# One step of a hybrid decoder on one core: other blocks for three pieces of MLP side work, other results with stored low parts, weights and cache in DRAM in the order of their loads

## The chip, the core and the metric

The kernel runs on one core of one Trainium2 chip. The metric is the device time of one launch in microseconds (us). Names of engines as in the profile: PE is TensorE, which multiplies matrices; PEld is its weight load; DVE is VectorE; ACT is ScalarE; POOL is GpSimd; SP only issues transfers. Each engine works through its own queue in program order, and so do the DMA queues that SP, ACT and POOL issue to. "Granted clock" is the share of full speed at which PE was allowed to run.

## What is computed

A layer of a decoder on 576 rows (512 of a prompt and 8 x 8 sampled ones) of 2048 features, in float32. Cut to what matters:

```python
q, k, v, logf, u = mixer_inputs(x, g_mix, w_in, b_f)       # rms_norm(x) @ w_in, split
attn = attention of the prompt, or over 2048 cached positions for the sampled rows
x = x + concat([rms_norm(attn), conv_heads(u)]) @ w_out
hid = square(relu(rms_norm(x, g_mlp) @ w_up))              # 2048 -> 8192
x = x + hid @ w_down                                       # 8192 -> 2048
gate = sigmoid(rms_norm(x, g_ple) @ w_ple_gate)
x = x + (pe @ w_ple) * gate
y = rms_norm(x, g_final)
```

The cache is paged: `page_table` says which physical page holds which positions.

## The kernel before

**Precision.** Every float32 operand is split into a high part (ACT, `split_hi`, L152) and a low part, the rest (DVE, `split_lo`, L155). A product is three matmuls: high x high, high x low, low x high.

**Two phases.** `phase1` does the input projection, both attentions, the convolution and, through `outproj`, the output projection. `WStream` brings its weights in loads of [128, 4, 128] (256 KB). The cache comes in pages, one load of 256 KB each for K and V (L833). `phase2` is the MLP and the gate, and the change lies there for the most part. Its weights come through `QStream`: loads of two quads (512 KB) or one into `w2r` by SP's queue, three ahead, with four buffers; then sums for DVE (L1832 to L1834), the high part `w2h` on ACT and the low part `w2l` on DVE, three buffers each. `prep(t + 2)` issues these for the block two ahead.

**Blocks and segments.** The MLP's pass is a list of blocks t, written out in program order. A block takes one quad of weights (256 x 256) against one slot: an operand of 256 features in high and low parts (`xs`). Up (g = 1) and down (g = 2) use a scheme with 7 products instead of 8 for 2 x 2 tiles (`PRODS`), so a block is 21 matmuls (L1607 to L1609) into 7 PSUM banks of 8. A segment is a run of blocks with one result:
- up: 32 results p of 8 blocks each, t = 0 to 255;
- down: 8 results p, 32 operands k, in segments of a few operands (`DOWN_FIRST`, `DOWN_PART`); the first are (2, 0), (2, 1) and (2, 2) with 3 blocks each from t = 256, 259 and 262, then (2, 3) with 4 from 265. t = 256 to 511;
- gate: first (3, 0) with both halves of the rows, 8 blocks of 24 matmuls, t = 512 to 519; then (4, 1) to (4, 7) and (5, 1) to (5, 7), one half each, 12 matmuls a block.

**A segment's end.** `combine_head` takes the first products out of PSUM (ACT L1725, DVE L1726 and L1727, ACT L1728) and `combine_tail` the others, at the next segment's first block (L1738 to L1741). The next segment's second product needs the bank that L1725 frees, its third that of L1726. A segment of the gate ends with `plain_end` (L1685), which needs the norm's row `rb`.

**Side work.** What follows a result (`fin_up`, `fin_down`, `fin_gate`) and the splitting of the next slots (`build` in `mk`) are generators in the queues of `Beside`. After each block `run` takes steps from queue 0 and then queue 1 as long as a credit lasts; the credit grows by the block's time and falls by the estimated DVE time of what is issued. A step that yields -n lets n blocks pass before the next. `flush` forces a generator to its end. `hook(t, fn)` runs `fn` right after block t's matmuls are issued and ahead of that block's `run`. A slot's `work` that has not run when its block comes is flushed ahead of the block's `prep`. Queue 2 holds only the last up result's `fin_up`; `nudge` takes one step of it per block in segments of down with p = 1 and 2, from block 259 on, ahead of the bank copies of a segment's last block.

**`fin_up`**: scale by the norm (L1380), Relu and Square (ACT L1383, L1384), the sums T (DVE L1693 to L1696), stores by POOL to `down_in` (L1320 to L1322). For the results in `down_lo` also `low_rows`: the low parts are made (`lr`) and stored to `dl`.

**Ready operands.** The first four operands of down are loaded with both parts: `down_in` into the high half, `down_lo` into the low half (L1507, L1508), 1 MB each. What is left is the high split on ACT alone (two activations). `DOWN_K` sets which up results these are; `build` waits `min(now - firstuse + 4, -1)`, and a hook three blocks ahead of the first use flushes what is left (L1541).

**The final norm** of the MLP's output: `squares` adds up `acc2`; `row_rsqrt` then sums over partitions on PE (L182), takes the reciprocal root in a chain of small DVE instructions (L184 to L188), and spreads it by PE (L192, 512 and then 64 columns) and ACT copies (L193) into `rb2`. It is a generator that yields ahead of each of the two spreads. `fin_down(7)` puts it into queue 1 as `norm`, and the end of block 519 flushes it.

Of the kernel before, what the change touches and what calls it, by code (L numbers as in the profile page):

```python
# [21 lines left out]
KT = 16  # L22
# [10 lines left out]
READY = 4  # L33
DOWN_K = (*range(8, 8 + READY), *range(8), *range(8 + READY, 32))
FIRST_LOADS = 2, 4, 5, 6, 3
# [110 lines left out]
class Kern:  # L146
# [71 lines left out]
    def build(self):  # L218
        tc, nc, a = self.tc, self.nc, self.a
        with ExitStack() as top:  # L220
# [8 lines left out]
            self.down_in = [dram.tile([128, 7, HR], F32, name=f"di{j}") for j in range(32)]  # L229
            self.down_lo = {j: dram.tile([128, 7, HR], F32R, name=f"dl{j}") for j in DOWN_K[:READY]}  # L230
            cst = top.enter_context(tc.tile_pool(name="cst", bufs=1))
# [17 lines left out]
    def phase1(self):  # L249
# [20 lines left out]

        wt = lambda t: [a["w_main"][t][:, j:j + 4, :] for j in range(0, KT, 4)]
        order = [("q", 4), ("q", 5), ("q", 6), ("q", 7), ("k", 0), ("v", 0), ("k", 1), ("v", 1)]
# [7 lines left out]
        for t in range(KT):  # L280
            srcs += [a["w_out"][t][:, j:j + 4, :] for j in range(0, KT, 4)]
        self.ws = WStream(nc, w1, srcs)
# [538 lines left out]
    def kv_load(self, i, m):  # L821

        nc, a = self.nc, self.a
        while len(self.kv[i]) < min(m, 128):
            n = len(self.kv[i])
            G, c, w, j = n // 32, n // 8 % 4, n // 2 % 4, n % 2
            p = n % self.KVN[i] >= self.KVA
            t = self.kvp[p].tile([128, 2, 4, 128], F32, name="kv"[i], tag="kv"[i] * 2, bufs=self.KVN[i] - self.KVA if p else self.KVA)
            for x in range(2):
                b, pg = (w, 2 * j + x) if i == 0 else (2 * j + x, w)  # L830
                e = (G % 2 * 4 + b) * NPG + c * 4 + pg
                r = nc.sync.value_load(self.pti[0:1, e:e + 1])
                nc.sync.dma_start(t[:, x].rearrange("p h c -> p (h c)"),  # L833
                                  a["cache_kv"][bass.ds(r, 1), G // 2, :, 512 * i:512 * i + 512].rearrange("o p c -> p (o c)"))
            self.kv[i].append(t)
# [417 lines left out]
    def plan(self):  # L1253
# [12 lines left out]
        for g, p, k0, k1 in segs:  # L1266
            parts = [(k, min(2, k1 - k)) for k in range(k0, k1, 2)]
            if (g, p) == (1, 0):
                parts = [(0, 2), (2, 2), (7, 1), (4, 2), (6, 1)]
            for k, m in parts:  # L1270
                loads.append((wsrc[g][p][:, k:k + m], m, g >= 3))
            self.orders.append([k + i for k, m in parts for i in range(m)])
# [93 lines left out]
    def phase2(self):  # L1366
# [12 lines left out]
        def fin_up(p, c, r, final):  # L1379
            V(c, c, rbb, ALU.mult)  # L1380
            yield EL(2 * NR)
            yield -1
            nc.scalar.activation(c, c, AF.Relu)  # L1383
            nc.scalar.activation(c, c, AF.Square)  # L1384
            yield -1
            c, T = yield from self.operands(c, None)
            self.stored(c, T, self.down_in[p])
            if p in self.down_lo:
                yield from self.low_rows(c, T, self.down_lo[p])

        def fin_down(p, c, r, final):

            if not final:
                nc.gpsimd.dma_start(self.x1[p], c, accum_op=ALU.add)
                yield 0
                return
            V(c, c, r, ALU.add)
            yield EL(2 * NR)
            nc.gpsimd.dma_start(self.x2[p], c)
            yield -1  # L1400
            yield from self.squares(p, c)
            if p == 7:
                self.last_norm = bg.add(1, self.norm(self.P_))

# [86 lines left out]
        def mk(g, j, t=None, queue=nc.gpsimd):  # L1491
# [48 lines left out]
            if ready or late:  # L1540
                hook(firstuse[2, j] - 3, lambda: bg.flush(h.work))  # L1541

# [13 lines left out]
        for n in range(RING, len(seq)):  # L1556
            g, j = seq[n]
            at = max(at, lastuse[(2, 32 - RING + (2 * j + 1) // 3) if g == 3 else seq[n - RING]])
            if g == 3:
                at = max(at, segend[lastseg[g - 1, j]] + 1)  # L1560
            hook(at, lambda g=g, j=j: mk(g, j))
        places = {j: self.xslot() for j in range(2, 7)}
        self.last = self.xslot()
# [12 lines left out]
        for t, (si, k) in enumerate(quadlist):  # L1576
# [49 lines left out]
            if i == n - 1:  # L1626
                if g > 1:
                    bg.flush_all(0)
                if slow:
                    r = pre[g](p, lastseg[g, p] == si)  # L1630
                if (g, p) == (3, 0):
                    bg.flush(self.last_norm)
                if recent[0]:
# [245 lines left out]


def feat(v):

# [3 lines left out]
def layout(inp):  # L1886
# [8 lines left out]
    d["p"] = C(p.T.reshape(2, 128, 576).transpose(1, 0, 2))  # L1895
    d["w_main"] = C(wm.reshape(16, 128, 40, 128).transpose(2, 1, 0, 3))
    d["w_f"] = C(w[:, 3072:3080].reshape(16, 128, 8).transpose(1, 0, 2))
    wo = g["w_out"][0].reshape(8, 2, 128, 16, 128)[list(OUT_ORDER)].reshape(16, 128, 16, 128)
    d["w_out"] = C(wo.transpose(2, 1, 0, 3))
    d["w_up"] = quads(g["w_up"][0], 32, 8)  # L1900
    d["w_down"] = np.ascontiguousarray(quads(g["w_down"][0], 8, 32)[:, :, list(DOWN_K)])
    d["w_gate"] = quads(g["w_ple_gate"][0], 8, 8)

# [3 lines left out]
    cv = g["cache_v"][0].reshape(-1, 128, 2, 4, 128)  # L1907
    d["cache_kv"] = C(np.stack([ck, cv], 3).transpose(0, 2, 1, 3, 4, 5)).reshape(-1, 2, 128, 1024)
    d["cache_logf"] = C(g["cache_logf"][0].reshape(-1, 1024))
# [51 lines left out]
```

## Time and profile before

| | |
|---|---|
| time, median of 3 runs | 2700.09 us (2697.12 to 2708.5) |
| the profiled execution's own time | 2699.89 us |
| its span, first to last instruction | 2698.1 us |
| mean granted clock | 0.996 |
| DVE, ACT, POOL busy | 76%, 43%, 19% |
| up: blocks 0 to 255 | from 1010.84 to 1737.99 us |
| down: blocks 256 to 511 | to 2466.35 us |
| (3, 0): blocks 512 to 519 | to 2498.46 us |

The rows on engines give start and length in us, engine, line, operation, what is written and read, and in brackets how long the engine had stood idle and what ended that. PE's matmuls are pipelined: one lasts 0.29 us in the rows, but they start some 0.13 us apart. The rows of stretches give, for each engine, its busy time and in parentheses its instructions. A mark "x2" stands for two instructions in a row, under the first one's shape.

### The profile page before, as it was taken

What the parts mean: (1) busy time and instruction counts of PE and PEld (TensorE: products, weight loads), DVE (VectorE), ACT (ScalarE), POOL (GpSimd) and SP (SyncE); (2) the same over time, 40 slices, a digit from 0 to 9 for tenths busy, and PEclk for the clock granted to TensorE, in tenths of its full rate; (3) what the DMA queues carried; (4) which work ended last, traced back from release to release, by engine and by line L of the source; (5) the groups of instructions that cost most, each with busy time, mean ns of one, the idle gap of its engine ahead of it and who ended that gap; (6) DMA issues with size and microseconds to landing.
All of it is one profiled execution on the core that took longest, in us unless ns stands there. A gap on an engine that the chain in (4) does not pass through costs nothing. (4 is left out here: it accounts for less than half of the span.)

```text
span 2698.1 us, 56355 instructions
## 1 busy us (share of the span) xinstructions
PE 2648.6 (98%) x21873; PEld 2561.3 (95%) x21873; DVE 2044.6 (76%) x3557; ACT 1160.0 (43%) x1704; POOL 517.3 (19%) x915
## 2 busy tenths in 40 slices
PE   9999999999999999999999999999999999999997
PEld 8899989888989999999999999999999999999997
DVE  6577777656554458888988888798888888888676
ACT  5222232335443335445544444454444444444554
POOL 2288786711000000001100000110000000000110
PEclk9999999999999999999999999999999999999999
DMA  5598888899755554445544444676565655656575
GB/s 204 174 303 295 292 295 289 294 308 321 260 191 162 173 195 161 156 142 165 165 144 141 138 146 142 237 204 186 166 186 153 182 163 172 181 174 219 185 240 168
DMA packets 240110, 544.38 MB, mean 202 GB/s; under 512 B 25729, under 2 KB 26754, under 8 KB 239842
## 3 DMA queue, kind: packets, MB, share of 16 engines
q1 hardware_dynamic: 171410, 330.95, 38.2%
q0 software_dynamic: 34896, 148.86, 17.4%
q10 hardware_dynamic: 33536, 60.96, 6.9%
q8 instruction: 171, 2.80, 0.4%
q14 instruction: 97, 0.79, 0.1%
HBM read 445.60 MB, written 95.09 MB: 200 GB/s over the span
## 5 line engine op out<-in xcount | busy, mean ns | idle before, releaser
L1607 PE MATMUL P<-xs,w2h 128*128 128x288 f32 x3584 | 1062.9, 297 | 8.1 <-DVE c L1726 3.8
L1608 PE MATMUL P<-xs,w2h 128*128 128x288 f32 x3584 | 1061.5, 296 | 2.0 <-DVE xs L155 2.0
L1609 PE MATMUL P<-xs,w2l 128*128 128x288 f32 x3584 | 1058.5, 295 | 2.5 <-DVE w2l L155 2.5
L152 ACT ACTIVATE w2h<-w2r 128x896 fp32r<-128x896 f32 (+1 forms) x632 | 560.3, 891 | 773.2 <-PE P L1608 459.1
L155 DVE TENSOR_TENSOR w2l<-w2r,w2h 128x896 fp32r<-128x896 f32 (+1 forms) x632 | 638.3, 1012 | 217.6 <-ACT w2h L152 215.5
L1607 PEld LDWEIGHTS P<-xs,w2h 128*128 128x128 f32 x3584 | 675.2, 188 | 14.1 <-DVE c L1726 7.0
L1608 PEld LDWEIGHTS P<-xs,w2h 128*128 128x128 f32 x3584 | 675.8, 189 | 3.4 <-DVE xs L155 3.2
L1609 PEld LDWEIGHTS P<-xs,w2l 128*128 128x128 f32 x3584 | 673.8, 188 | 3.9 <-DVE w2l L155 3.9
L498 PE MATMUL U<-xh,whi 128*128 128x288 f32 x1792 | 397.7, 303 | 0.1
L498 PE MATMUL U<-xl,whi 128*128 128x288 f32 x1792 | 381.4, 294 | 0.9 <-DVE xl L337 0.9
L498 PE MATMUL U<-xh,wlo 128*128 128x288 f32 x1792 | 381.7, 294 | 0.0
L498 PEld LDWEIGHTS U<-xh,whi 128*128 128x128 f32 x1792 | 285.9, 188 | 18.8 <-issue 16.3
L126 ACT ACTIVATE whi<-wraw 128x512 fp32r<-128x512 f32 x224 | 140.7, 629 | 355.1 <-PE U L498 295.2
L498 PEld LDWEIGHTS U<-xl,whi 128*128 128x128 f32 x1792 | 287.0, 188 | 1.8 <-DVE xl L337 1.7
L498 PEld LDWEIGHTS U<-xh,wlo 128*128 128x128 f32 x1792 | 286.9, 188 | 0.0
L132 DVE TENSOR_TENSOR wlo<-wraw,whi 128x512 fp32r<-128x512 f32 x224 | 158.3, 708 | 115.0 <-ACT whi L126 114.4
L1045 DVE SCALAR_TENSOR_TENSOR y<-ue,cv,y 128x512 f32<-128x512 f32 x240 | 184.7, 769 | 5.3
L1832 DVE TENSOR_TENSOR w2r<-w2r 128x512 f32<-128x512 f32 (+1 forms) x273 | 178.0, 652 | 5.1 <-DMA w2r<-in_w_down 5.1
L1046 POOL TENSOR_SCALAR cvt<-us,cv 128x64 f32<-128x64 f32 x240 | 165.4, 689 | 22.3
L1679 PE MATMUL P<-xs,w2l 128*128 128x288 f32 x512 | 151.6, 296 | 1.0 <-DVE w2l L155 0.9
L1677 PE MATMUL P<-xs,w2h 128*128 128x288 f32 x512 | 152.0, 297 | 0.0
L1678 PE MATMUL P<-xs,w2h 128*128 128x288 f32 x512 | 151.4, 296 | 0.0
(390 smaller groups left out, 2772.5 us busy)
## 6 DMA issues: line engine op xcount, KB each, us to landing
k<-in_cache_kv SPq DMA_DIRECT2D x256, 256.0 KB, 4.7
v<-in_cache_kv SPq DMA_DIRECT2D x256, 256.0 KB, 4.9
w2r<-in_w_up SPq DMA_DIRECT2D x127, 512.0 KB, 4.0
w2r<-in_w_down SPq DMA_DIRECT2D x112, 512.0 KB, 4.2
wraw<-in_w_main ACTq DMA_DIRECT2D x156, 256.0 KB, 5.0
xs<-di POOLq DMA_DIRECT2D x32, 1008.0 KB, 6.1
w2r<-in_w_gate SPq DMA_DIRECT2D x60, 512.0 KB, 4.5
x<-c POOLq DMA_DIRECT2D x48, 576.0 KB, 6.0
```

Of the source, the lines that this page charges most:

```text
L132: self.nc.vector.tensor_tensor(lo, self.raw.pop(c), f(hi), ALU.subtract)
L152: self.nc.scalar.activation(out, in_, AF.Copy, **kw)
L155: self.nc.vector.tensor_tensor(out, in_, f(hi), ALU.subtract)
L498: self.nc.tensor.matmul(u[:, r, :HR], w, x[:, r * HR:(r + 1) * HR], start=first and n == 0, stop=last and n == 2)
L1045: nc.vector.scalar_tensor_tensor(y, ue[:, j:j + NPR], w, y, ALU.mult, ALU.add)
L1046: nc.gpsimd.tensor_scalar(t, us[:, :, j:j + 8], w, None, ALU.mult)
L1607: nc.tensor.matmul(o, hi[:, ia, :], s.hi[:, ib, :], start=(i == 0), stop=False)
L1608: nc.tensor.matmul(o, hi[:, ia, :], s.lo[:, ib, :], start=False, stop=False)
L1609: nc.tensor.matmul(o, lo[:, ia, :], s.hi[:, ib, :], start=False, stop=(i == n - 1))
L1677: nc.tensor.matmul(o, hi[:, ia, :], s.hi[:, kh, rows], start=first and kh == 0, stop=False)
L1679: nc.tensor.matmul(o, lo[:, ia, :], s.hi[:, kh, rows], start=False, stop=last and kh == 1)
L1832: lambda: V(w[:, :, 4:6, :], w[:, :, 0:1, :].broadcast_to([128, m, 2, 128]), w[:, :, 1:3, :], ALU.add),
```

## The change

Five edits:
1. The four up results with a stored low part, which are the first four operands of down, are 8, 10, 12 and 14 in place of 8 to 11. The columns of `w_down` follow.
2. The hook that flushes the third ready operand (j = 2) stands two blocks ahead of its first use in place of three.
3. `fin_up` of result 31 has one more yield between the scaling and Relu. Since `nudge` takes one step per block, everything behind it moves by one block; the stores are then issued by the flush at block 264.
4. The final norm is no longer in queue 1. Three hooks after the fourth, sixth and seventh block of (3, 0) take one step of `row_rsqrt` each: sums, chain and `dg`; 512 columns and copy; 64 columns and copy. The flush at the end of block 519 is gone.
5. `w_main`, `w_out`, `w_up`, `w_gate` and the cache lie in DRAM so that what one load fetches is one piece. Sizes, number and destinations of the loads stay.

```diff
-DOWN_K = (*range(8, 8 + READY), *range(8), *range(8 + READY, 32))
+DOWN_LO = (8, 10, 12, 14)
+DOWN_K = (*DOWN_LO, *(k for k in range(32) if k not in DOWN_LO))
...
-            self.down_lo = {j: dram.tile([128, 7, HR], F32R, name=f"dl{j}") for j in DOWN_K[:READY]}
+            self.down_lo = {j: dram.tile([128, 7, HR], F32R, name=f"dl{j}") for j in DOWN_LO}
...
-        wt = lambda t: [a["w_main"][t][:, j:j + 4, :] for j in range(0, KT, 4)]
+        wt = lambda t: [a["w_main"][t][j] for j in range(KT // 4)]
...
-            srcs += [a["w_out"][t][:, j:j + 4, :] for j in range(0, KT, 4)]
+            srcs += [a["w_out"][t][j] for j in range(KT // 4)]
...
-                                  a["cache_kv"][bass.ds(r, 1), G // 2, :, 512 * i:512 * i + 512].rearrange("o p c -> p (o c)"))
+                                  a["cache_kv"][bass.ds(r, 1), G // 2 * 2 + i].rearrange("o p c -> p (o c)"))
...
-                loads.append((wsrc[g][p][:, k:k + m], m, g >= 3))
+                w = wsrc[g][p]
+                loads.append((w[:, k:k + m] if g == 2 else w[k // 2][:, k % 2:k % 2 + m], m, g >= 3))
...
             V(c, c, rbb, ALU.mult)
             yield EL(2 * NR)
             yield -1
+            if p == 31:
+                yield -1
             nc.scalar.activation(c, c, AF.Relu)
...
             yield from self.squares(p, c)
-            if p == 7:
-                self.last_norm = bg.add(1, self.norm(self.P_))
...
-                hook(firstuse[2, j] - 3, lambda: bg.flush(h.work))
+                hook(firstuse[2, j] - (2 if j == 2 else 3), lambda: bg.flush(h.work))
...
+        gen = None
+
+        def last_norm():
+
+            nonlocal gen
+            if gen is None:
+                bg.flush(fin_of[2, 7])
+                gen = self.row_rsqrt(self.P_, self.aux, self.buf("dg")[:, 0, :], self.acc2, self.rb2, 2048.0)
+            next(gen, None)
+
+        for i in (3, 5, 6):
+            hook(seg0[lastseg[3, 0]] + i, last_norm)
...
-                if (g, p) == (3, 0):
-                    bg.flush(self.last_norm)
...
+def pairs(q):
+
+    n, p, k, b, c = q.shape
+    return np.ascontiguousarray(q.reshape(n, p, k // 2, 2, b, c).transpose(0, 2, 1, 3, 4, 5))
...
-    d["w_main"] = C(wm.reshape(16, 128, 40, 128).transpose(2, 1, 0, 3))
+    d["w_main"] = C(wm.reshape(4, 4, 128, 40, 128).transpose(3, 0, 2, 1, 4))
...
-    d["w_out"] = C(wo.transpose(2, 1, 0, 3))
-    d["w_up"] = quads(g["w_up"][0], 32, 8)
+    d["w_out"] = C(wo.reshape(4, 4, 128, 16, 128).transpose(3, 0, 2, 1, 4))
+    d["w_up"] = pairs(quads(g["w_up"][0], 32, 8))
...
-    d["w_gate"] = quads(g["w_ple_gate"][0], 8, 8)
+    d["w_gate"] = pairs(quads(g["w_ple_gate"][0], 8, 8))
...
-    d["cache_kv"] = C(np.stack([ck, cv], 3).transpose(0, 2, 1, 3, 4, 5)).reshape(-1, 2, 128, 1024)
+    d["cache_kv"] = C(np.stack([ck, cv], 3).transpose(0, 2, 3, 1, 4, 5)).reshape(-1, 4, 128, 512)
```

## The prediction

> **What bounds the kernel now.** I read the page first, then a table of busy time by stretches whose borders are starts of MLP blocks, then the waits, then single engines in order of time at the places the change touches.
>
> ```profile
> span 2698.1 us, 56355 instructions
> PE 2648.6 (98%) x21873; PEld 2561.3 (95%) x21873; DVE 2044.6 (76%) x3557; ACT 1160.0 (43%) x1704; POOL 517.3 (19%) x915
> PEclk9999999999999999999999999999999999999999
> ```
>
> TensorE (PE) is the bound. What a change can win is its idle time, its time at a lower granted clock, and the pace of its matmuls. The stretches (us; then busy time and instructions of PE, PEld, DVE, ACT, POOL; granted clock, DMA share, GB/s):
>
> ```profile
> 200.00:600.00 400.00, 391.53 (x4239) 353.85 (x4238) 279.21 (x536) 115.42 (x241) 262.26 (x471) 1.00 0.88 295
> ...
> 1107.67:1240.47 132.80, 132.80 (x1010) 132.80 (x1009) 115.59 (x180) 64.60 (x75) 10.19 (x19) 1.00 0.45 144
> 1240.47:1311.88 71.41, 69.28 (x506) 67.16 (x505) 63.44 (x100) 37.15 (x45) 8.07 (x15) 1.00 0.55 176
> 1334.79:1737.99 403.20, 403.20 (x3027) 403.20 (x3025) 343.44 (x539) 191.11 (x218) 33.31 (x62) 1.00 0.47 152
> 1737.99:1782.13 44.14, 39.68 (x275) 37.91 (x274) 38.05 (x68) 21.22 (x30) 4.89 (x7) 0.96 0.80 249
> ...
> 1913.18:2167.98 254.80, 254.80 (x1913) 254.80 (x1912) 220.46 (x348) 118.48 (x141) 18.56 (x26) 1.00 0.63 178
> 2466.35:2498.46 32.11, 28.92 (x209) 27.80 (x207) 19.51 (x39) 10.40 (x17) 2.14 (x4) 0.94 0.65 221
> 2498.46:2514.12 15.66, 14.68 (x98) 14.21 (x98) 9.53 (x15) 10.37 (x17) 1.62 (x3) 0.90 0.36 107
> ```
>
> A block of up or down is 21 matmuls. The stretch from 1107.67 holds six results of 8 blocks: 132.80 / 48 = 2.767 us a block. The one from 1334.79 holds 18 results: 403.20 / 144 = 2.800. Both have no idle time and the full clock; the matmuls are merely 131.8 or 133.3 ns apart. Between them, where results 10 to 12 run, lie stalls. So there is a fast and a slow pace, 0.034 us a block apart, and the pace changed where PE had stalled. In down it is slow too (254.80 / 91 blocks = 2.800).
>
> **Part 1: low parts of results 8, 10, 12, 14.** Stalls first. ACT's rows while results 9 and 10 run, then DVE's:
>
> ```profile
> 1231.17 1.17 ACT L152 ACTIVATE lr<-T 128x1152 fp32r<-128x1152 f32 x1 [2.81 <-DVE T L1696]
> ...
> 1255.22 1.17 ACT L152 ACTIVATE lr<-T 128x1152 fp32r<-128x1152 f32 x1 [2.81 <-DVE T L1696]
> 1256.30 1.77 ACT L152 ACTIVATE w2h<-w2r 128x896 fp32r<-128x896 f32 x2
> ```
>
> ```profile
> 1257.26 1.09 DVE L155 TENSOR_TENSOR w2l<-w2r,w2h 128x896 fp32r<-128x896 f32 x1 [1.47 <-ACT w2h L152]
> ```
>
> ACT works in order. At 1255.22 the split of T for the low part of result 9 sits ahead of the next weight split (w2h), waits 2.81 us for DVE's T, and PE then lacks w2l. The same split, with the same wait, ran for result 8 at 1231.17, inside the undisturbed stretch that ends at 1240.47. The difference is the start of fin_up: the last steps of result 8's low part fall into the next result's first two blocks and push fin_up(9) one block back, and so on for 10 and 11. With every second result, fin_up(9) is still pushed back but has no low part, and its queue is empty before result 10's begins. All four low parts then run as result 8's does. Their work (1.17 us for the split shown) stays, covered by PE's blocks; were that cover gone, each would cost what a result loses now, 1.7 us (below, 5.0 / 3).
>
> Price: results 10 to 12 take 71.41 us against 24 x 2.767 = 66.4, so 5.0. Result 13 runs from 1311.88 to 1334.79, 22.91 against 22.13: 0.8. If nothing stalls, I see no reason for the pace to change, and the 144 blocks from 1334.79 take 398.4 in place of 403.2: 4.8. Together 10.6 us. Bounds: 4.7 if the slow pace comes anyway (94.32 us for results 10 to 13 against 32 x 2.800 = 89.6); nothing if a low part stalls wherever it stands. I take 10.6, since the fast pace held 48 blocks without a stall, one low part among them.
>
> **Part 2: third ready operand.** The diff moves a forced flush from block 255 to block 256.
>
> ```profile
> 1732.51 0.95 ACT L152 ACTIVATE w2h<-w2r 128x896 fp32r<-128x896 f32 x1
> 1737.19 1.98 ACT L152 ACTIVATE xs<-xs 128x864 fp32r<-128x864 f32 x2 [3.73 <-DMA xs<-di]
> 1739.08 0.93 ACT L152 ACTIVATE w2h<-w2r 128x896 fp32r<-128x896 f32 x1
> 1739.92 0.39 ACT L1725 ACTIVATE c<-P 128x288 f32<-128x288 f32 x1
> ```
>
> The stall is real: the split of the operand waits for its load, and w2h and the copy that frees a PSUM bank (L1725) queue behind it. But the operand's own wait in `build` is over one block after its first step, and the credit of block 254 then issues it: in the rows it stands ahead of the w2h of block 255 (1739.08; 1732.51 is block 254's). The flush finds nothing left to do at either block. So I take zero: the stall keeps its part of the 7.7 us by which the first 13 blocks of down (44.14) exceed 36.4. Bounds: a gain of 2.0, the split's length, if it really moves; a loss of 0.2, because a faster PE meets the same landing 7 x 0.034 us earlier.
>
> **Part 3: last up result.** Its Relu and Square move from block 261 to 262, the sums T from 262 and 263 to 263 and 264; its stores still follow in block 264, before the bank copy, so POOL's queue keeps its order, and down needs result 31 only much later.
>
> ```profile
> 1756.65 1.79 ACT L152 ACTIVATE w2h<-w2r 128x896 fp32r<-128x896 f32 x2 [6.40 <-PE P L1609]
> 1758.35 1.15 ACT L1383 ACTIVATE c<-c 128x1152 f32<-128x1152 f32 x1
> ...
> 1760.60 0.39 ACT L1725 ACTIVATE c<-P 128x288 f32<-128x288 f32 x1
> ```
>
> ```profile
> 1758.79 0.40 PE L1609 MATMUL P<-xs,w2l 128*128 128x288 f32 x1 [0.40 <-DVE w2l L155]
> 1761.05 0.61 PE L1607 MATMUL P<-xs,w2h 128*128 128x288 f32 x1 [1.86 <-ACT c L1725]
> ```
>
> ```profile
> 1759.18 1.08 DVE L155 TENSOR_TENSOR w2l<-w2r,w2h 128x896 fp32r<-128x896 f32 x1
> 1761.03 0.46 DVE L1726 TENSOR_TENSOR c<-c,P 128x288 f32<-128x288 f32 x1 [0.76 <-ACT c L1725]
> ...
> 1767.94 1.09 DVE L155 TENSOR_TENSOR w2l<-w2r,w2h 128x896 fp32r<-128x896 f32 x1 [0.46 <-ACT w2h L152]
> ...
> 1771.48 0.45 DVE L1726 TENSOR_TENSOR c<-c,P 128x288 f32<-128x288 f32 x1
> ```
>
> Without the two activations L1725 runs at 1758.35, 2.25 us earlier. What is late next is DVE: the third product of block 262 needs L1726, which follows w2l and cannot start before 1760.2. From there DVE is busy but for the 0.46 until L1726 of the next result, now at 1771.48; it has the same work before it afterwards, so that comes only its 0.8 us of removed wait earlier. PE, ahead by more, waits at block 265 instead, about 2 us by these rows. I take a gain of 0.8. Bounds: 3.0 if DVE does not hold PE back; a loss of 0.8 if the stall at block 265 costs a stretch of half clock (1.6, below).
>
> **Part 4: final norm in steps.** It now runs between the eighth block of the (3, 0) segment and the next:
>
> ```profile
> 2491.94 1.17 PE L182 MATMUL P<-ones,acc 128*128 128x2 f32 x10
> 2496.30 2.40 PE L192 MATMUL P<-dg,ones 128*128 128x512 f32 x4 [3.19 <-DVE dg L186]
> ```
>
> ```profile
> 2479.85 1.45 ACT L152 ACTIVATE xs<-xs,vecs 128x576 fp32r<-128x576 f32 x2
> 2482.41 0.63 ACT L152 ACTIVATE w2h<-w2r 128x512 fp32r<-128x512 f32 x1 [1.11 <-PE P L1678]
> 2482.94 1.43 ACT L152 ACTIVATE xs<-xs,vecs 128x576 fp32r<-128x576 f32 x2
> ...
> 2498.41 0.71 ACT L193 ACTIVATE rb<-P 128x512 f32<-128x512 f32 x2 [8.98 <-PE P L192]
> ```
>
> ```profile
> 2479.87 0.69 DVE L155 TENSOR_TENSOR w2l<-w2r,w2h 128x512 fp32r<-128x512 f32 x1 [2.45 <-ACT w2h L152]
> 2480.66 1.55 DVE L1536 SCALAR_TENSOR_TENSOR xs<-xs,vecs 128x576 fp32r<-128x576 f32 x2
> ...
> 2493.15 0.17 DVE L184 TENSOR_SCALAR rrm<-P 128x5 f32<-128x5 f32 x1 [2.98 <-PE P L182]
> ...
> 2496.17 0.25 DVE L188 TENSOR_SCALAR dg<-ident,rrs 128x64 f32<-128x64 f32 x1
> ```
>
> Now: 25.6 us of blocks (8 x 3.20) plus 6.5, and the low clock costs 0.10 x 15.66 = 1.6 in the next segment. Removed: PE's wait of 3.19 and both stretches of low clock. Three new waits take its place, since two queues run in order.
> Block 515 (the fourth) ends at 2466.35 + 4 x 3.20 = 2479.15, and DVE can start 1.21 later, as L184 does after L182's start. Its chain of 3.27 us (2493.15 to 2496.42) then holds w2l and the operand split L1536 of the sixth block until 2483.6; with 0.7 for w2l and 0.8 for the split's first half that is ready at 2485.1, and PE, which is there at 2483.5, waits 1.5.
> After block 517 come the 512 columns of L192 and ACT's copy L193. Behind that copy on ACT stands the split of the seventh operand (now at 2482.94, after the same w2h), which PE needs at once. From the end of L192: hardly 0.1 to the copy (L184 starts 0.04 after L182's end), 0.5 of the pair's 0.71 for it, 0.8 for the split's first half (DVE's row starts 0.81 after ACT's), 0.8 for DVE's half: 2.2 us.
> After block 518, with the copy of 64 columns (0.2), the same: 1.9.
> New total: 25.6 + 1.0 (L182) + 1.1 (L192 at full clock, half of 2496.30 to 2498.46) + 1.5 + 2.2 + 1.9 = 33.3, against 32.1 + 1.6 = 33.7: a gain of 0.4. Bounds: 6.0 if all three are hidden; a loss of 2.8 if two of them bring the low clock (2 x 1.6). I stay near the lower middle, as both queues are plain in the rows.
> The clock: the stall of 0.40 + 1.86 at 1761 lies in a stretch with 0.96 of the clock, 44.14 x 0.04 / 0.5 = 3.5 us at half, and PE's row at 1761.05 shows the longer matmul; half of 3.5, some 1.6, is what I count for one such event. [...]
>
> **Part 5: DRAM in load order.** Destinations, sizes (2 KB runs) and the number of transfers stay; only the DRAM stride between partitions goes (8 KB for w_main and w_out, 16 KB for w_up and w_gate, 4 KB for the cache). In up, down and gate DMA has room (0.45 to 0.65). The attention phase is fuller:
>
> ```profile
> PE O L896 <- DMA v<-in_cache_kv: 4.9, 9, 1.5
> ```
>
> ```profile
> q1 hardware_dynamic: 171410, 330.95, 38.2%
> ```
>
> A packet takes 0.382 x 16 x 2698.1 / 171410 = 96 ns in the mean. If reading in order makes it faster, PE's 4.9 us of waits for V shrink, no more. No row shows these loads in order, so the bounds are a gain of 4.9 and, if packets get as much longer as they could get shorter, a loss of 2; I take 2 for the gain. [...]
>
> **Sum.** 10.6 + 0 + 0.8 + 0.4 + 2 = 13.8 us. The profiled execution took 2699.89 us (1.8 outside its span), 0.2 under the median of 2700.09. 2699.9 - 13.8 = 2686.1; small second gains (a fast pace that lasts into down is worth up to 217 x 0.034 = 7.4) let me put 2685.5.
>
> **Rivals.**
> *The slow pace comes anyway.* For: in down it came after every small stall. Then part 1 gives 4.7: 2692.
> *The steps clear the stalls.* Parts 2 to 4 give most of 2.0, 3.0 and 6.0: with parts 1 and 5 2677. Against: the queues above.
> *DRAM order is nothing.* Parts 1, 3 and 4 alone: 2688. For: packets keep their size. [...]
> *Slower, through DRAM order.* If 256 KB in one piece make the 16 DMA engines meet at one place in memory, packets lengthen. At 0.88 share and 96 ns the engines are full at 109 ns; from there, all of the some 600 us of cache reading stretches. At 114 ns it is 4.6%, 27 us, net +15: 2715. No row speaks for it.
>
> **How the numbers follow.** Forecast (2681 to 2690): 0.50. Slow pace: 0.22. Stalls cleared: 0.14. DRAM nothing: 0.10. Slower: 0.04. Range 2675 to 2697: it takes in the second, third and fourth case with 2 us around. A measurement of this kernel tells some 0.5% (13.5 us) from no change, so the border is 2686.6. Below lie 0.6 of the forecast, the cleared stalls and a little of the others: 0.50. Within: 0.45. Slower: 0.05.
>
> **What will show it.** Right: no ACT wait for T with PE idle between results 10 and 13, and 2.77 us a block up to down; the wait for the third operand's load before down still there; DVE ending a wait of about 2 us at block 265; three waits in (3, 0), ended by L1536 and ACT, and no 3.2 us one. Wrong: 2.80 in up; a first block of down without a stall; (3, 0) near 28 us; V waits as before, or more.

## The result, and the profile after

The changed kernel takes 2698.15 us (median of 20 runs, 2686.10 to 2707.32), the one before, run beside it, 2704.14 (20 runs, 2696.01 to 2709.59). The ratio is **0.9974, 95% interval 0.9964 to 0.9985**: 7 us gained by the ratio (6 by the medians) where 14 were forecast. The time lies 1.2 us outside the predicted range and 12.7 above the forecast of 2685.5; some 4 us of that are the kernel before itself, at 2704.14 beside these runs and at 2700.09 in the three that the prediction went by. A second set of 12 runs gave 0.9981 (0.9969 to 0.9993). The profiled execution took 2698.77 us, 1.1 less than the one of before.

Page of the changed kernel: span, busy time, granted clock in 40 slices.

```profile
span 2697.0 us, 56364 instructions
PE 2652.2 (98%) x21873; PEld 2568.7 (95%) x21873; DVE 2044.4 (76%) x3557; ACT 1160.0 (43%) x1704; POOL 518.3 (19%) x915
PEclk9999999999999999999999999999999999999998
```

Stretches of the changed kernel, its own block starts as borders (columns as in the prediction):

```profile
1108.93:1243.34 134.41, 134.41 (x1011) 134.41 (x1010) 115.80 (x181) 64.55 (x75) 10.19 (x19) 1.00 0.42 143
1243.34:1310.54 67.20, 67.20 (x507) 67.20 (x506) 61.06 (x97) 33.22 (x39) 6.46 (x12) 1.00 0.50 167
1332.93:1736.13 403.20, 403.20 (x3026) 403.20 (x3025) 346.62 (x545) 192.87 (x222) 34.90 (x65) 1.00 0.46 156
1736.13:1781.07 44.94, 40.78 (x276) 39.46 (x274) 38.15 (x68) 21.31 (x30) 4.88 (x7) 0.92 0.80 242
1913.16:2009.99 96.83, 96.83 (x737) 96.83 (x736) 85.77 (x135) 46.30 (x55) 7.73 (x11) 1.00 0.66 190
2029.57:2166.77 137.20, 137.20 (x1032) 137.20 (x1030) 116.63 (x185) 62.90 (x75) 9.99 (x14) 1.00 0.63 178
2463.35:2498.39 35.04, 30.55 (x208) 28.93 (x207) 20.23 (x43) 10.93 (x18) 2.14 (x4) 0.95 0.56 202
2498.39:2512.69 14.30, 13.18 (x99) 12.71 (x98) 8.73 (x13) 9.83 (x15) 1.59 (x3) 1.00 0.36 117
```

The stalls of results 10 to 12 are gone: their 24 blocks take 67.20 us with TensorE (PE) busy throughout, in place of 71.41. But 67.20 / 24 is 2.800, and so are the blocks ahead (134.41 / 48), which before ran at 2.767. In down it is the other way: 35 blocks from 1913.16 at 2.767, slow before. The first 13 blocks of down (44.94) and the last piece beside the norm with the one behind it (35.04 + 14.30 = 49.34) are longer than before (44.14 and 47.77). The granted clock is lower than before in the first (0.92 for 0.96), not in the others (0.95 and 1.00 for 0.94 and 0.90).

The waits of the changed kernel list for V:

```profile
PE O L897 <- DMA v<-in_cache_kv: 1.2, 3, 0.7
```

Matched by the number of the matmul, the two traces part as follows (after minus before, us; each line adds the stretch named):

| up to | time before | step | sum |
|---|---|---|---|
| end of attention | 769.7 | -5.4 | -5.4 |
| start of up | 1010.8 | +6.4 | +1.1 |
| block 112 | 1334.8 | -2.9 | -1.9 |
| block 269 | 1782.1 | +0.8 | -1.1 |
| block 512 | 2466.4 | -1.9 | -3.0 |
| block 528 | 2514.1 | +1.6 | -1.4 |

Of the five edits only the DRAM order of `w_out` touches what stands behind the second line, the output projection. What took 6.4 us there is the first thing to find.

### The profile page after: what moved, and what is told of

Same layout as the page of the kernel before. It is cut to its first block, busy times and chain, and to the rows that moved or that the text cites. A ratio compares the mean times of both kernels' runs of the same rounds, so it can differ in the third digit from the quotient of the medians.

```text
span 2697.0 us, 56364 instructions
## 1 busy us (share of the span) xinstructions
PE 2652.2 (98%) x21873; PEld 2568.7 (95%) x21873; DVE 2044.4 (76%) x3557; ACT 1160.0 (43%) x1704; POOL 518.3 (19%) x915
## 3 DMA queue, kind: packets, MB, share of 16 engines
q1 hardware_dynamic: 171410, 330.95, 37.6%
## 4 chain that ended last, share of the span: by engine, by line
PE 84%; issue 6%; DVE 5%; DMA 2%; ACT 1%; POOL 0%; SPq 0%; ACTq 0%; DVEq 0%; POOLq 0%
PE U L499 18%; PE P L1621 17%; PE P L1622 17%; PE P L1623 16%; PE P L1690 2%; PE P L1691 2%; PE P L1689 2%; PE D L866 2%; PE O L897 2%; PE U L1136 1%; DVE w2l L156 1%; DMA wraw<-in_w_main 1%; PE S L759 1%; PE S L739 1%; DMA w2r<-in_w_down 0%
```

## The experiments

The runs stood beside the kernel before on the same chip; ratios are to it. "Theory A" is the account from the two profiles: part 1 worth 4.7 us, part 2 nothing, part 3 hardly anything, part 4 a loss, part 5 about 5, and a pace that each execution draws for itself.

### The pace: the same program twice, and stalls put in

hook_only is the kernel before with part 2 alone:

```diff
-                hook(firstuse[2, j] - 3, lambda: bg.flush(h.work))
+                hook(firstuse[2, j] - (2 if j == 2 else 3), lambda: bg.flush(h.work))
```

> The kernel before with the third ready operand's hook moved by a block, alone. The instructions of every engine come out in the same order as before, so this is a second look at the kernel before. Theory A (the pace is drawn afresh at each stall, in each execution): the ratio is 1 within 0.001, and in the profile some stretches have another pace than before had them: the out-projection behind 770 us (fast only in the profile before, slow in five others), blocks 25 to 79 (2.767 before, 2.800 in after, last_only and norm_only), blocks 304 to 350, 352 to 406 and 409 to 462 (all 2.800 before). TensorE's wait for v, 4.9 us before and 2.3 to 2.9 in three other profiles with the old DRAM order, comes out at 2 to 3 us. Rival P (the pace belongs to the program): the same stretches have the same pace as in the profile before, throughout.

Measured: 2702.83 us, ratio 1.0000 (0.9986 to 1.0013). Three stretches of its profile: the output projection, blocks 309 to 350, blocks 358 to 406.

```profile
830.00:1000.00 170.00, 170.00 (x1277) 170.00 (x1276) 75.97 (x119) 54.13 (x80) 11.90 (x22) 1.00 0.51 168
1901.09:2017.29 116.20, 116.20 (x885) 116.20 (x884) 102.85 (x161) 55.58 (x66) 9.16 (x13) 1.00 0.66 189
2036.65:2172.22 135.57, 135.57 (x1032) 135.57 (x1030) 116.69 (x184) 62.96 (x75) 9.99 (x14) 1.00 0.64 180
```

The same work in the profile before:

```profile
830.00:1000.00 170.00, 170.00 (x1310) 170.00 (x1309) 77.81 (x121) 55.23 (x82) 11.90 (x22) 1.00 0.51 169
1893.58:2011.18 117.60, 117.60 (x884) 117.60 (x883) 103.06 (x161) 55.55 (x66) 9.16 (x13) 1.00 0.65 186
2030.78:2167.98 137.20, 137.20 (x1031) 137.20 (x1030) 116.66 (x185) 62.93 (x75) 9.98 (x14) 1.00 0.63 178
```

hook_only issues the same instructions as the kernel before, in the same order on every engine. One instruction stream, then, and 1277 matmuls in 170 us of output projection against 1310 (133.1 ns and 129.8), 116.20 us for 42 blocks against 117.60, all at the full clock with PE never idle. Rival P falls: the pace does not belong to the program. The DRAM order falls as the cause of the slow output projection too, since hook_only has the old one. (TensorE's wait for V came out at 3.5 us, above the 2 to 3 expected.)

low_only is the kernel before with part 1 alone.

```diff
-DOWN_K = (*range(8, 8 + READY), *range(8), *range(8 + READY, 32))
+DOWN_LO = (8, 10, 12, 14)
+DOWN_K = (*DOWN_LO, *(k for k in range(32) if k not in DOWN_LO))
```

> The kernel before with the low parts of results 8, 10, 12 and 14 dropped early, alone. Theory A (equal pace): the waits at blocks 85 to 87, 88, 93 to 96, 101 to 104 are gone, and blocks 80 to 111 take 89.6 us at 2.800 us a block or 88.5 at 2.767, against 94.3 before; the run is 4.7 us faster (ratio 0.9983), give or take what pace is drawn. Theory P (the prediction on record: without those waits the fast pace of 2.767 lasts up to block 255): blocks 32 to 255 take 619.8 us, and the run is 10 us faster (ratio 0.9963). The profile after had the slow pace from block 24, drawn at the stall of block 24, so this run's pace from there tells whether it belongs to the edit.

Measured: 2695.68 us, ratio 0.9988 (0.9976 to 1.0000). Blocks 32 to 255 in its profile:

```profile
1111.22:1730.96 619.74, 619.74 (x4707) 619.74 (x4706) 543.54 (x850) 302.70 (x350) 53.71 (x100) 1.00 0.49 156
```

619.74 us in this one execution: the prediction's case to a tenth, where the changed kernel has 627.2. The twelve runs don't bear that case out, though: 3.2 us by the ratio (0 to 6.5), not the 10 of theory P and a little under theory A's 4.7. Without stalls the pace of block 25 held to the end of up in every one of the seven profiles with part 1 and no stall put in; it was 2.767 in two of them and 2.800 in five. In the five kernels that still had the stalls, blocks 112 to 255 ran at 2.800 each time.

nine_stalls is low_only with a stall forced nine times:

```diff
+        def stall():
+            for _ in range(10):
+                nc.scalar.activation(scr, scr, AF.Copy)
+        for t in range(40, 241, 25):
+            hook(t, stall)
```

> The kernel before with its low parts dropped early (low_only), and ten copies of a scratch tile on ScalarE behind blocks 40, 65, 90, 115, 140, 165, 190, 215 and 240, each set some 6 us long, so that a weight's split comes late and TensorE stalls by one to a few us nine times where low_only had no stall at all. Theory A (the pace of a stretch is drawn at a stall): between the nine stalls some stretches run at 2.767 us a block and others at 2.800, with at least two changes, and none away from a stall. Rival P (the pace of these blocks is set once, at block 24, and the stalls only happened to stand where it changed): one pace in all ten stretches. The time itself says nothing here; the nine stalls add what they last.

Measured: one run, 2735.60 us. Blocks 45 to 63 and 169 to 190 of its profile:

```profile
1157.22:1210.42 53.20, 53.20 (x401) 53.20 (x400) 45.80 (x73) 24.48 (x29) 3.76 (x7) 1.00 0.47 149
1520.36:1581.22 60.86, 60.86 (x465) 60.86 (x463) 54.00 (x84) 30.40 (x35) 4.83 (x9) 1.00 0.48 151
```

The run began at 2.767, went to 2.800 at the stall behind block 40 (53.20 / 19) and back to 2.767 at the one behind 165 (60.86 / 22 = 2.766), and kept its pace through the other seven. Theory A holds, with the least number of changes that it asked for, two in nine: a stall was an occasion for the pace to change here, not a coin toss.

after_again is the changed kernel, not edited.

> The changed kernel once more, unchanged, beside best. Theory A (the pace is drawn afresh): a ratio of 0.996 to 0.9985, and a profile in which some stretches have another pace than in the first profile of the changed kernel (blocks 25 to 255 at 2.800, 303 to 350 at 2.767, 352 to 406 at 2.800, 408 to 462 at 2.767), while the places that the program sets come out as before: block 256 at 5 to 6.5 us, blocks 512 to 527 at 49 to 51, TensorE's wait for v at 1 to 2.5. Rival P: the same paces.

Measured: 2701.89 us, ratio 0.9981 (0.9969 to 0.9993). Blocks 352 to 406 now 2.767, 409 to 462 now 2.800, 269 to 294 now 2.767, block 256 6.83 us, blocks 512 to 527 50.9, V waits 1.5. The program's own places came back, block 256 a little above the 5 to 6.5 us expected. Of the paces, those of blocks 25 to 255 and 304 to 350 came back, those of the three stretches just named did not, in the very same program. The table gathers all profiles but that of nine_stalls (f: 2.767 a block, or 129.8 ns a matmul in the output projection; s: 2.800, 133 ns).

| profile | output projection | 25-79 | 112-255 | 304-350 | 352-406 | 409-462 |
|---|---|---|---|---|---|---|
| before | f | f | s | s | s | s |
| hook_only | s | f | s | f | f | s |
| dram_only | s | f | s | f | f | f |
| last_only | s | s | s | f | f | s |
| norm_only | s | s | s | f | f | f |
| low_only | s | f | f | s | s | s |
| no_norm | s | f | f | f | f | s |
| norm_mended | s | s | s | f | f | f |
| third_moved, best, after_again | s | s | s | f | f | s |
| after | s | s | s | f | s | f |

The profile before was the odd one: the only fast output projection (from matmul 8100 to 9600 of the trace it gained 4.9 us on each of the others), and, as in low_only, slow in all three stretches of down. The other 1.5 of the 6.4 us stand ahead of matmul 8100: in the changed kernel a wait of 2.0 us on VectorE was followed by a stretch of half clock at 798.04 us, in the kernel before not. One reservation: no single program was seen at both paces in blocks 25 to 79. But up to block 40 all thirteen runs issue the same instructions in the same order (nine_stalls one memset more), and six went fast from block 25, seven slow.

### DRAM order alone

dram_only is the kernel before with part 5's lines of the diff and no others.

> The kernel before with the reordered DRAM tensors alone. Theory A (the order itself brings V in sooner): the idle time of TensorE before the first matmul on v, 4.9 us in 9 groups in the profile before and 1.2 in 3 after, comes out at 1 to 2 us; the matmuls up to 765 us run 4 to 6 us ahead of those before, the run is 3 to 6 us faster (ratio 0.998 to 0.999) unless the pace draws differently. Rival B (the V waits differ from execution to execution, and the order is worth nothing): the waits stay at 4 to 5 us, and the ratio is 1.000 within 0.0015. The prediction on record had 2 us, between bounds of a 4.9 us gain and a 2 us loss.

Measured: 2698.72 us, ratio 0.9991 (0.9981 to 1.0001): 2.4 us, where theory A had 3 to 6. Waits for V:

```profile
PE O L896 <- DMA v<-in_cache_kv: 1.6, 5, 0.7
```

The same wait in low_only, which has the old order:

```profile
PE O L897 <- DMA v<-in_cache_kv: 2.9, 7, 1.0
```

So both theories had a part. With the old order the wait was 4.9, 4.5 (nine_stalls), 3.5, 2.9, 2.5 and 2.3 us in six profiles, mean 3.4; with the new one 2.5, 1.7, 1.6, 1.5, 1.2, 1.1 and 1.0 in seven, mean 1.5. By the starts of matmuls 900 and 6600 (123 and 660 us before), the seven gained 3.9 to 6.1 us on the profile before over this stretch; of the other five with the old order, nine_stalls lost 3.5 and four gained 0.7 to 2.9. The groups don't overlap and the means differ by 4.2 us: the order gains about that much, and part of the 4.9 us of before was a bad draw. Only 1.9 of the 4.2 are idle time in these waits; the rest are longer distances between matmuls, among them the stretches of half clock that followed such waits in hook_only (at 503.88 us) and nine_stalls (502.60 and 567.45). The interval of the runs alone would not have shown it. Cache and `w_main` were reordered together; which of the two counts was not tried.

### The head of down: parts 3 and 2

last_only is the kernel before with part 3's two lines (`if p == 31: yield -1`).

> The kernel before with the last up result's head moved to the other block, alone. Theory A: the waits of blocks 259 and 262 (0.69 and 4.26 us over the pace before) become one of 2.4 us at block 265 and one of 1 us at block 262, perhaps with a stretch of half clock behind it, and blocks 259 to 268 are 0.5 to 1.5 us shorter; the ratio is 0.9995 to 1.000, which the runs can't tell from 1. Rival N (the move itself makes the wait of block 256 longer, 5.42 us before and 6.37 after): block 256 takes over 6 us here too, and blocks 256 to 268 come out no shorter than the 44.1 us before.

Measured: 2700.78 us, ratio 1.0004 (0.9994 to 1.0013); blocks 259 to 268 32.55 us (33.19 before), blocks 256 to 268 43.13. That fits theory A, but not steadily: over all profiles blocks 256 to 268 take 44.1 to 44.6 us without part 3 and 43.1 to 45.2 with it (third_moved and best left out), means 44.3 and 44.2. The edit is worth nothing that these profiles can show. Why shows in the changed kernel, TensorE's row at block 265 and VectorE's (DVE) ahead of it:

```profile
1769.31 0.40 PE L1621 MATMUL P<-xs,w2h 128*128 128x288 f32 x1 [1.74 <-DVE c L1738]
```

```profile
1766.94 1.08 DVE L156 TENSOR_TENSOR w2l<-w2r,w2h 128x896 fp32r<-128x896 f32 x1
1767.95 0.45 DVE L1707 TENSOR_TENSOR T<-c,T 128x288 f32<-128x288 f32 x1
1768.43 0.46 DVE L1708 TENSOR_TENSOR T<-T,c 128x288 f32<-128x288 f32 x1
1768.81 0.45 DVE L1738 TENSOR_TENSOR c<-c,P 128x288 f32<-128x288 f32 x1
```

DVE runs without a gap and reaches the bank sum (L1738) at 1768.81; PE has waited 1.74 us for it. The stall has moved three blocks on, and half clock follows it here as it followed the one at block 262 before.

third_moved is the changed kernel with the wait of the third operand's generator put off too:

```diff
-                    yield min(bg.now - 1000 - firstuse[2, j] + 4, -1)
+                    yield min(bg.now - 1000 - firstuse[2, j] + (2 if j == 2 else 4), -1)
```

> The changed kernel with the third ready operand's split really put off by two blocks: besides the hook, the generator that makes it gives way until the later time. Theory A (the hook's move does nothing since the generator's own due time issues the split with block 254, ahead of the copies of block 256): the split leaves its place, the wait ahead of block 256 shrinks, and block 256 takes 2.8 to 4.5 us where it took 5.05 to 6.68 in six profiles; blocks 256 to 268 fall from 43.1 to 44.9 us to 40 to 42, with 2 to 3.5 us gained (ratio to the kernel before about 0.9963). Rival B (the same wait turns up where the third operand is first used, a block or two later): blocks 256 to 268 stay at 43 to 45 us.

ScalarE (ACT) around block 256, changed kernel first:

```profile
1735.26 1.98 ACT L153 ACTIVATE xs<-xs 128x864 fp32r<-128x864 f32 x2 [3.66 <-DMA xs<-di]
1737.15 0.93 ACT L153 ACTIVATE w2h<-w2r 128x896 fp32r<-128x896 f32 x1
1737.98 0.39 ACT L1737 ACTIVATE c<-P 128x288 f32<-128x288 f32 x1
```

The same in third_moved:

```profile
1738.07 0.95 ACT L153 ACTIVATE w2h<-w2r 128x896 fp32r<-128x896 f32 x1 [1.86 <-PE P L1622]
1738.93 0.39 ACT L1737 ACTIVATE c<-P 128x288 f32<-128x288 f32 x1
...
1741.72 1.96 ACT L153 ACTIVATE xs<-xs 128x864 fp32r<-128x864 f32 x2
```

In the changed kernel the split still stands ahead of w2h and the bank copy and still waits 3.66 us for its load, as before: the moved hook had found nothing to do. Put off in earnest, it runs behind the copy with no wait. Block 256 takes 2.80 us, blocks 256 to 268 42.03 (44.94), and the run 2692.26 us, ratio 0.9956 (0.9941 to 0.9971). Theory A holds; the ratio is better than 2.9 us make it, over nine runs that spread by 12.6.

### The final norm: alone, taken out, set otherwise

norm_only is the kernel before with part 4's lines alone, no_norm the changed kernel without them.

> The kernel before with the final norm in steps, alone. Theory A: the last MLP piece that runs beside it (blocks 512 to 519) and the first gate piece (blocks 520 to 527) take 49 to 50 us together, against 47.8 before and 49.3 after: the one stall of 6.5 us at block 519 turns into three of 1.2 to 2 us at blocks 517, 518 and 519 with a stretch of half clock behind them, so the step costs 1 to 2 us (ratio 1.0005). Rival N (the prediction on record: the three stalls are together 0.4 us shorter than the one): 47.4 us, ratio 0.9998. The runs can't tell these two apart; the two pieces in the profile can, and the half clock shows in the granted clock of that stretch.

> The changed kernel without the final norm in steps. Theory A: blocks 512 to 527 go back from 49.3 us to 47 to 47.8 (46.99 to 47.78 in four profiles with the old norm, 49.33 and 50.87 in two with the steps), so it is 1.5 to 3 us faster than the changed kernel: ratio to the kernel before about 0.9965, where the changed kernel's is 0.9974. Rival N (the prediction on record: the steps gain 0.4 us): ratio no better than 0.9974, blocks 512 to 527 over 49 us for another reason.

Measured: norm_only 2702.40 us, ratio 1.0004 (0.9994 to 1.0014); no_norm 2700.88, 0.9981 (0.9967 to 0.9995). The times don't show the loss: no_norm's ratio is no better than the changed kernel's, as rival N had it, and theory A's 0.9965 lies just outside its interval. The two pieces in the profiles tell: blocks 512 to 527 take 46.8 to 47.8 us in six profiles with the old norm (no_norm 47.0; mean 47.4; nine_stalls, left out, 47.7) and 49.3 to 50.9 in four with the steps (norm_only 50.9, above the 49 to 50 expected; mean 50.1). The steps cost 2.8 us. In the changed kernel, PE's waits there, then ACT's rows:

```profile
2482.00 0.40 PE L1690 MATMUL P<-xs,w2h 128*128 128x288 f32 x1 [1.25 <-DVE xs L1538]
2487.53 0.40 PE L1689 MATMUL P<-xs,w2h 128*128 128x288 f32 x1 [1.35 <-ACT xs L153]
2488.38 0.40 PE L1690 MATMUL P<-xs,w2h 128*128 128x288 f32 x1 [0.46 <-DVE xs L1538]
2492.86 0.40 PE L1689 MATMUL P<-xs,w2h 128*128 128x288 f32 x1 [0.97 <-ACT xs L153]
2493.71 0.40 PE L1690 MATMUL P<-xs,w2h 128*128 128x288 f32 x1 [0.45 <-DVE xs L1538]
```

```profile
2486.22 0.60 ACT L194 ACTIVATE rb<-P 128x512 f32<-128x512 f32 x1 [5.07 <-PE P L193]
2486.71 1.43 ACT L153 ACTIVATE xs<-xs,vecs 128x576 fp32r<-128x576 f32 x2
...
2491.92 0.22 ACT L194 ACTIVATE rb<-P 128x64 f32<-128x64 f32 x1 [3.26 <-PE P L193]
2492.04 1.43 ACT L153 ACTIVATE xs<-xs,vecs 128x576 fp32r<-128x576 f32 x2
```

ACT sat idle 5.07 us in front of the copy L194, and the operand's split, which before ran at 2482.94 (a row of the prediction), stood behind it; then PE waits for the split's halves, first ACT's, then DVE's. With the wait at block 525 (1.0 us here), which every profile has, PE waits 5.6 us in blocks 512 to 527, and 4.2 in the kernel before. Then comes half clock, in norm_only at length:

```profile
2490.00:2494.00 4.00, 2.19 (x10) 1.85 (x10) 2.15 (x3) 2.44 (x4) 0.00 (x0) 0.85 0.84 332
2494.00:2498.00 4.00, 3.35 (x19) 3.21 (x17) 0.00 (x0) 0.62 (x2) 0.00 (x0) 0.72 0.00 0
```

These stretches are not what sets the steps apart: with the old norm each profile has one or two of them as well, and over blocks 512 to 527 the clock is 0.93 in the kernel before and 0.97 in the changed one.

norm_mended sets the changed kernel's steps so that no split stands behind one that waits long:

```diff
+        t30 = seg0[lastseg[3, 0]]
+        hook(t30 + 4, norm_step)
+        hook(t30 + 5, norm_step)
...
+            if t == t30 + 3:
+                norm_step()
```

The step at t30 + 3 makes the sums and DVE's chain ahead of block 515's matmuls; the hooks give both spreads to PE behind block 516 and both copies to ACT behind block 517.

> The changed kernel with the final norm's steps set otherwise: the sums and the chain on VectorE ahead of block 515's matmuls, both spreads by TensorE behind block 516, both copies by ScalarE behind block 517's matmuls, so that no split of a gate operand stands behind a step that waits. Theory A (the steps of the change cost since the chain on VectorE and the copies on ScalarE stand in front of the gate operands' splits, and the half clock follows the stalls): no stall over 1.3 us in blocks 512 to 519, no half clock there, blocks 512 to 519 take 27 to 30 us (35.0 in the changed kernel, 32.1 before), blocks 512 to 527 take 42 to 45 (49.3, 47.8): 5 to 7 us faster than the changed kernel, ratio to the kernel before about 0.995. Rival B (the gate's weights or the head of the last result set the end there): blocks 512 to 527 stay above 46 us, with the waits on a weight's split or on the last result.

Measured: 2692.87 us, ratio 0.9958 (0.9942 to 0.9974); blocks 512 to 519 28.27 us, blocks 512 to 527 42.58, the clock at 1.00, no wait of PE over 0.3 us in blocks 512 to 519. ACT's rows:

```profile
2478.67 0.71 ACT L1585 ACTIVATE rb<-P 128x512 f32<-128x512 f32 x2 [0.36 <-PE P L1581]
2479.27 1.44 ACT L153 ACTIVATE xs<-xs,vecs 128x576 fp32r<-128x576 f32 x2
```

A split still stands behind the copies, but ACT waits 0.36 us ahead of them in place of 5.07 and 3.26. Theory A holds.

### Both mends

best has the edits of third_moved and norm_mended together.

> The changed kernel with both mends: the third operand's split really put off by two blocks, and the final norm's steps set so that no gate split stands behind one. Theory A (the two stalls are independent, so what each mend took away alone adds): block 256 takes 2.8 us and blocks 256 to 268 41 to 43 (44.9 in the changed kernel), blocks 512 to 527 42 to 43 (49.3), together 9 to 10 us less than the changed kernel; the ratio to the kernel before is 0.993 to 0.995, and the median 8 to 11 us below after_again's. Rival B (one mend gives its gain back in the stage between, by a stall or by another pace drawn): less than 5 us below after_again.

Measured: 2686.29 us (6 runs, 2683.41 to 2691.05), **ratio 0.9928 (0.9914 to 0.9941)**, 15.6 us below after_again's median, more than the 8 to 11 expected. In the two profiles it is 11.7 us (spans 2686.2 and 2697.9), of which 3.9 lie in blocks 256 to 268 and 8.3 in blocks 512 to 527; the rest of the medians' difference is not accounted for; the runs of the changed kernel spread by 16 us. Against the first profile of the changed kernel the two places are 3.7 and 6.8 us shorter, where each mend alone took 2.9 and 6.8: the mends add, as theory A had it. Its stretches: blocks 256 to 268, 512 to 519, 520 to 527.

```profile
1738.51:1779.72 41.21, 38.67 (x275) 37.89 (x274) 36.56 (x66) 20.73 (x27) 4.88 (x7) 0.96 0.87 265
2459.64:2487.90 28.26, 28.03 (x209) 27.32 (x207) 20.55 (x42) 10.94 (x18) 2.14 (x4) 1.00 0.68 234
2487.90:2502.20 14.30, 13.17 (x99) 12.71 (x97) 8.73 (x13) 9.83 (x15) 1.60 (x3) 1.00 0.45 150
```

PE is busy 28.03 of 28.26 us where it had been busy 30.55 of 35.04, and the clock is full.

## Why the prediction was wrong

Its sum was 13.8 us. With each term at the size that the profiles gave it, the sum is 6.2 + 0 + 0 - 2.8 + 4.2 = 7.6 us or 0.28%, inside the measured interval of 0.15 to 0.36%. This is bookkeeping and no test: the ratios of the runs with one part each add up to 3.5 us, give or take some 6.7 (their intervals added in squares).

- **Part 1, mis-sized by some 4 us.** The mechanism was right: the low part's split was what stalled, and with every second result no wait was left from block 25 to 255. The sum failed at "If nothing stalls, I see no reason for the pace to change". True, but the pace that then lasts is drawn at the stall of block 24, and I had seen one draw of it. With that draw slow, blocks 32 to 255 go from 631.6 us to 627.2, 4.4 less; with it fast, from 630.3 to 619.7, 10.6 less. It was fast in two profiles of the seven: 4.4 + 2/7 x 6.2 = 6.2. (By the six of all thirteen it is 7.3, and the sum above 8.7.) The rival "The slow pace comes anyway" was the case in the other five: it priced the gain at 7.9 us, and its 2692 lies under 2698 by the 4 us of the reference and by part 4. Its ground, that in down the slow pace came after every small stall, was a misreading: before ran blocks 266 to 294 at 2.767, right behind the stalls of 256 to 265.
- **The reference.** The median of three runs, 2700.09 us, lay 4 us under that of twenty. And I took the profiled execution, 0.2 us below the three's median, as a fair sample stretch by stretch. It was not: 4.9 us lucky in the output projection, slow in down, some 2 us unlucky in the attention against four of the other five profiles with the old order (nine_stalls was 3.5 worse still). A total at the median says nothing of its parts.
- **Part 2, right.** The flush found nothing to do, as hook_only's unchanged order of instructions shows; that the stall is real is shown by third_moved, which takes it away (block 256 from 6.37 to 2.80 us).
- **Part 3, right in place, its gain not confirmed.** The wait came at block 265, ended by DVE, as the prediction had it, at 1.74 us for "about 2". For the 0.8 us, blocks 259 to 268 are 0.65 us shorter in the changed kernel (32.54 for 33.19), but 0.2 in the means over all profiles (32.3 for 32.5, third_moved and best left out). The clock of 0.92 for 0.96 is a second stretch of half clock; it stands behind block 256, ahead of what part 3 moves.
- **Part 4, wrong in sign.** The three places and their releasers were right (L1538, which is L1536 before, then ACT's copies), and the waits even shorter than worked out: 1.25, 1.81 and 1.42 us for 1.5, 2.2 and 1.9. What failed was the clock: the sum took out both old stretches of half clock and left the new ones to the bounds ("I stay near the lower middle"). They came: one here, which costs (1 - 0.95) x 35.04 = 1.8 us, two in norm_only and after_again. So in the means no clock was saved (5.1 us at half with the steps, 5.4 with the old norm), the waits add up to more than the old norm's (5.6 us for 4.2), and a wait cost more than it lasted: the 1.25 us at the row at 2482.00 cost 1.41, the 0.97 at 2492.86 cost 1.12, by the starts of the matmuls around them.
- **Part 5, right in sign, too small:** 4.2 us for 2, near the bound of 4.9. Packets became little shorter (queue q1 held the engines for 37.6% of the span, 38.2 before); what the rows show is V landing earlier, for 1.9 of the 4.2.

The rival that the DRAM order is nothing had for it that packets keep their size. By it dram_only should have waited for V as long as the old order; waits of 1.5 us for 3.4 in the means (single profiles touch: 2.5 in third_moved, 2.3 in last_only) and an attention stretch whose two groups don't overlap speak against it for these loads of 256 KB, if by little.

## What to carry to other kernels

Before costing a change against one profile, read the same program's profile twice: what differs between the two is not yours to gain. When a pass is in order, a step that is cut in pieces must be placed by what stands behind each piece on each engine; here much the same steps cost 2.8 us in one place and saved 4.8 in another. And a hook that forces work is no way to delay it: whoever issues first sets the time.

## What the runs showed of the hardware

**Two paces.** PE busy, clock 1.00, the same instructions, and a block takes 2.767 or 2.800 us, the latter for 231 blocks on end in the changed kernel (25 to 255). The distances between the starts of its 21 matmuls (ns, each the mean over 8 blocks) repeat to 1 ns or so:

```
before, blocks 60 to 67:    133 132 133 136 136 131 132 132 131 133 130 126 131 134 132 131 132 129 131 131 132
before, blocks 150 to 157:  130 140 134 136 145 139 136 130 132 133 133 132 138 126 131 129 131 129 132 133 131
```

The first pattern, give or take 1 ns, is that of the changed kernel in blocks 303 to 350 and 408 to 462 too, the second that of the changed kernel in blocks 112 to 255 and of before in 303 to 406. The pace changed at stalls for the most part. In before it was 2.767 up to block 84 and 2.800 from block 105 to 255, with the stalls of results 10 to 12 between, and 2.767 again behind block 265, which took 3.24 us; the stall of block 24 (3.97 us in both profiles) was followed by 2.767 in before and by 2.800 in the changed kernel. Two changes stand where PE shows no wait, both from 2.767 to 2.800: in before at block 295 (2.85 us), in the changed kernel at block 351 (2.79 us). What locks a cycle was not found out, nor a way to choose it; the stretches of the table come to over 15 us (4.9, and 55 + 144 + 156 blocks at 0.034), of the 20 or so by which runs of one program differ.

**Half clock after short stalls.** In half clock the starts of matmuls in the changed kernel lie 240 ns apart (2494.71 to 2497.83), for some 0.13 us before and after. The trace's record of the granted clock has it at 0.50 from 1760.91 us for 3.41 us and from 2494.78 for 6.83 in the kernel before, and in the changed kernel for 3.41 us each from 798.04, 1740.12, 1770.84 and 2494.47; in both, one more stretch runs past the end. The starts lie on a grid of 3.413 us, 215 steps apart in before, 276, 9 and 212 in the changed kernel. In the changed kernel half clock followed the waits of 1.73 us at block 256 and 1.74 at block 265, in before the 1.86 at block 262, but not the 1.81 at block 256. With up and down cut into pieces by that grid, PE was idle for 2.12 us in the piece ahead of the half clock in before, for 1.86 and 1.74 in those of the changed kernel, for 1.81 in the one at block 256 in before that none followed, and for less than 1 us in every other piece of the two profiles. What decides between 1.74 and 1.81 is not shown. The 1.86 us at block 262 fall into one piece in before, but are cut in two in hook_only (1.17 and 1.06 us idle), where the clock stayed at 1.00:

```profile
1757.50:1760.91 3.41, 1.29 (x8) 0.84 (x6) 2.59 (x4) 3.38 (x6) 0.00 (x0) 1.00 0.57 182
1760.91:1764.32 3.41, 3.27 (x13) 3.28 (x14) 3.16 (x7) 1.22 (x3) 0.09 (x1) 0.50 0.54 154
```

```profile
1763.40:1766.82 3.42, 2.25 (x16) 1.81 (x14) 2.56 (x5) 3.30 (x4) 0.00 (x0) 1.00 0.91 254
1766.82:1770.23 3.41, 2.35 (x18) 2.35 (x19) 2.51 (x7) 2.15 (x4) 0.00 (x0) 1.00 0.54 150
1770.23:1773.64 3.41, 3.41 (x28) 3.41 (x27) 3.41 (x7) 0.00 (x0) 2.00 (x3) 1.00 0.42 45
```
